# Transposing attention probabilities by DMA: the strided groups of three pairs of heads in mixer A

## The chip, the cores and the metric

The kernel runs on one core of one Trainium2 chip. The metric is the device time of one execution in microseconds (us), lower is better.

## The reference

A two-layer bidirectional encoder on x (1, 512, 1024) in float32. Layer 0 uses mixer A, layer 1 mixer B (latent attention); each mixer is followed by a squared-ReLU MLP of width 4096. The change is in mixer A, a mixture of dilated window attentions. One projection gives q, k and v for three groups (window, dilation) with eight heads of 128 each; the groups' outputs are merged by their softmax denominators:

```python
qkv = (h @ w_qkv).reshape(B, S, 3, N_GROUPS, A_HEADS, A_HEAD_DIM)
for g, (window, dil) in enumerate(((128, 1), (512, 4), (2048, 16))):
    q = rope(rms_norm(qkv[:, :, 0, g], q_gain[g]), S)
    k = rope(rms_norm(qkv[:, :, 1, g], k_gain[g]), S)
    o, lse = dilated_group(q, k, qkv[:, :, 2, g], window, dil)   # softmax(q k) v in the window
    ...
wts = jax.nn.softmax(jnp.stack(lses, 0), axis=0)
o = sum(wts[g][..., None] * outs[g] for g in range(3))
return o.reshape(B, S, A_WIDTH) @ w_o
```

## The kernel before, in words

Everything of one layer stays in the core's SBUF, with the 512 positions in four tiles of 128 partitions. The engines are TensorE (PE: matmuls and transposes into PSUM), VectorE (DVE), ScalarE (ACT), GpSimd (POOL) and SyncE (SP, which here issues DMA transfers). No order is written out by hand: a scheduler places each engine's instructions by a timeline of its own, and buffers come from pools, where a tile with a tag waits until one of the tag's buffers is free.

Projections are fp32 by parts. A weight tile is loaded raw (L146, L148), ScalarE takes the high part (whi, L158), VectorE the low part (wlo, L159), and TensorE adds three products (L186, the tiles called acc). These projections are the bulk of TensorE's work.

Mixer A handles its eight heads in four pairs b = 0 to 3. For a pair and a group, `project_in(b, g)` projects q and k of two heads. Each of its four tiles of 128 positions is squared (L138), rotated on VectorE (L278, L281), scaled (L130, POOL, L286, L287), and then transposed without TensorE: ScalarE splits its 32-bit words into low and high halves (L289), a DMA transpose issued by SP turns the 16-bit tile of 128 x 1024 (L292) into a tile xT (two buffers), and ScalarE puts the halves together again in qkT (L297). `scores(b, g)` then multiplies q and k (L578 and L582 for group 0, L589 for the strided groups 1 and 2), adds masks (L585, L594), takes maxima (L597, L598) and exponentials (L600), which leaves the probabilities P for each group and head.

When all three groups of a pair are there, `finish` runs `merge`, which works out the weights of the three groups with small matmuls (L644, L669) and multiplies the P tiles by them on VectorE (L675), and then `pv` for head h = 0 and 1. `pv` needs each P tile transposed, so that the key positions lie on the partitions. Before the change TensorE does that for all groups (L125, four 128x128 blocks into one PSUM tile tp). VectorE copies the tiles of groups 1 and 2 out (L685), ScalarE those of group 0 (L692), into tiles pT with four buffers:

```python
pT = aw.tile([P, 512], F32, tag="pT", name=nm("pT"), bufs=4)
V.tensor_copy(pT, tp)
```

Then TensorE multiplies them with the values: L699 for groups 1 and 2 (vt), L703 for group 0 (v0n and v0c), all into one PSUM tile sco, which VectorE copies to oT (L705). The values were written to DRAM earlier and are loaded pair by pair by `v_load` on SP: vt (L629), v0n (L605), and v0c in eight small transfers (L608).

So that TensorE has projections to do meanwhile, `finish(b)` is called after `project_in(b + 1, 0)`; the scheduler mixes the two, and the scores of the next pair's group 0, as its timeline has it. The last pair (b = 3) is finished apart, with the last head's value projection (`v_last`) and the start of the output projection as company; the tiles oA that the latter needs are split on ScalarE at L744.

Of the kernel before, what the change touches and what calls it, by code (L numbers as in the profile page):

```python
# [10 lines left out]
F32 = mybir.dt.float32  # L11
F32R = mybir.dt.float32r
U16 = mybir.dt.uint16
# [5 lines left out]
P = 128  # L19
S = 512  # L20
NT = S // P
# [3 lines left out]
HA = 8  # L25
# [63 lines left out]
def encoder_kernel(ctx: ExitStack, tc: tile.TileContext, x, norm_mix, norm_ffn, a_w_qkv, a_q_gain, a_k_gain,  # L89
                   a_w_o, b_w_in, b_q_a_gain, b_w_qb, b_kv_a_gain, b_w_kvb, b_q_gain, b_k_gain, b_w_o,  # L90
                   ffn_w1, ffn_w2, consts, out):
    nc = tc.nc
    V, A, G, PE = nc.vector, nc.scalar, nc.gpsimd, nc.tensor
# [3 lines left out]
    def nm(s):  # L97
        uid[0] += 1
        return f"{s}_{uid[0]}"
# [14 lines left out]
    tp_p = ctx.enter_context(tc.tile_pool(name="tp_p", bufs=2, space=PSUM))  # L114
# [9 lines left out]
    def transpose(o, i):  # L124
        PE.transpose(o, i, ident)  # L125
# [420 lines left out]
    with tc.tile_pool(name="apool", bufs=1, reuse_waits="tile") as ap_, \  # L546
# [19 lines left out]
        def scores(b, g, qkT, Pt, stats):  # L566

            m, den, nb = stats
            for h in range(2):
                qT, kT = qkT[:, h], qkT[:, 2 + h]  # L570
                for part in range(2 if g == 0 else 1):
                    sc = sc_p.tile([P, 512], F32, tag="sc", name=nm("sc"))
                    pt = Pt[g][h]
                    if g == 0:
                        for ii in range(2):
                            i = 2 * part + ii
                            q_i = qT[:, i * P:(i + 1) * P]
                            PE.matmul(sc[:, ii * 256:ii * 256 + 128], lhsT=q_i, rhs=kT[:, i * P:(i + 1) * P],  # L578
                                      start=True, stop=True)
                            segs = bass.AP(tensor=kT.tensor, offset=kT.offset + SEG_A[i],  # L580
                                           ap=[list(kT.ap[0]), [SEG_B[i] - SEG_A[i], 2], [1, 64]])
                            PE.matmul(sc[:, ii * 256 + 128:ii * 256 + 256], lhsT=q_i, rhs=segs, start=True, stop=True)  # L582
                        sv = sc.rearrange("p (i k) -> p i k", i=2)
                        pv = pt[:, 2 * part:2 * part + 2, :]
                        V.tensor_tensor(pv, sv, m0[:, 2 * part:2 * part + 2, :], op=ALU.add)  # L585
                        cols = range(2 * part, 2 * part + 2)
                    else:
                        for r in range(NT):
                            PE.matmul(sc[:, r * P:(r + 1) * P], lhsT=qT[:, r * P:(r + 1) * P],  # L589
                                      rhs=kT[:, r * P:(r + 1) * P], start=True, stop=True)  # L590
                        sv = sc.rearrange("p (i k) -> p i k", i=NT)
                        pv = pt
                        mk = (m1 if g == 1 else m2).unsqueeze(1).broadcast_to([P, NT, P])
                        V.tensor_tensor(pv, sv, mk, op=ALU.add)  # L594
                        cols = range(NT)
                    c0, c1 = cols[0], cols[-1] + 1
                    V.tensor_reduce(m[:, g, h, c0:c1], pv, axis=AX.X, op=ALU.max)  # L597
                    V.tensor_scalar(nb[:, g, h, c0:c1], m[:, g, h, c0:c1], -SCALE_A, None, op0=ALU.mult)  # L598
                    for c in cols:
# [77 lines left out]
        def pv(b, h, Pt, vt, v0n, v0c):  # L677
            pts = []
            hs = slice(DH * h, DH * h + DH)
            for g in (1, 2):  # L680
                tp = tp_p.tile([P, 512], F32, tag="tp", name=nm("tp"))
                for r in range(NT):
                    transpose(tp[:, r * P:(r + 1) * P], Pt[g][h][:, r])
                pT = aw.tile([P, 512], F32, tag="pT", name=nm("pT"), bufs=4)
                V.tensor_copy(pT, tp)  # L685
                pts.append(pT)
            for part in range(2):
                tp = tp_p.tile([P, 512], F32, tag="tp", name=nm("tp"))
                for i in range(NT):
                    transpose(tp[:, i * P:(i + 1) * P], Pt[0][h][:, i, part * P:(part + 1) * P])  # L690
                pT = aw.tile([P, 512], F32, tag="pT", name=nm("pT"), bufs=4)
                A.activation(pT.rearrange("p (i r j) -> p i r j", i=NT, r=NT),  # L692
                             tp.rearrange("p (i j r) -> p i r j", i=NT, r=NT), AF.Copy)
                pts.append(pT)
            o = sc_p.tile([P, 512], F32, tag="sc", name=nm("sco"))
            ov = o.rearrange("p (r m) -> p r m", r=NT)
            for r in range(NT):
                for g in (1, 2):
                    PE.matmul(o[:, r * P:(r + 1) * P], lhsT=vt[:, r, g - 1, hs], rhs=pts[g - 1][:, r * P:(r + 1) * P],  # L699
                              start=(r == 0 and g == 1), stop=False, skip_group_check=True)  # L700
            for i in range(NT):
                for part, vv in ((0, v0n), (1, v0c)):
                    PE.matmul(ov[:, :, 32 * i:32 * i + 32], lhsT=vv[:, i, hs], rhs=pts[2 + part][:, i * P:(i + 1) * P],  # L703
                              start=False, stop=(i == NT - 1 and part == 1), skip_group_check=True)
            V.tensor_copy(oT[:, 2 * b + h], o)  # L705
# [7 lines left out]
        def turned():  # L713
            return aw.tile([P, 8, P], U16, tag="xT", name=nm("xT"))
# [15 lines left out]
        for b in range(HA // 2):  # L730
            Pt = [[ap_.tile([P, NT, 256 if g == 0 else P], F32, tag=f"P{g}{h}", name=nm("P")) for h in range(2)]
                  for g in range(NG)]
# [223 lines left out]
    if True:  # L956
        with tc.tile_pool(name="bpool", bufs=1, reuse_waits="tile") as bp, \
# [205 lines left out]
            pend, tail, nxt, pT, pTs = [], [], None, None, None  # L1163
            plan = {2: [(kv_chunk, 0)], 3: [(kv_chunk, 1), (kv_chunk, 2)], 4: [(kv_chunk, 3), (q_chunk, 0)],
                    5: [(q_chunk, 1)], 6: [(q_chunk, 2)], 7: [(q_chunk, 3)]}
            for s_ in range(HB * NT + lag):
                p, c = divmod(s_, 8)
# [4 lines left out]
                if s_ >= lag:  # L1172
                    d, h2, r2, f = pend.pop(0)
                    if r2 == 0:
                        if pTs is None:
                            pTs = x16.tile([P, 2, NT, S], F32, tag="x16", name="pTs")
                        pT = pTs[:, h2]
# [54 lines left out]
```

## Time and profile before

| | us |
|---|---|
| median of 3 timed runs | 1414.49 (1411.01, 1414.49, 1415.36) |
| the profiled execution | 1413.8 |
| its span | 1412.0 |
| TensorE busy in the span | 1374.6 (97%) |
| VectorE busy | 940.3 (67%) |
| ScalarE busy | 801.3 (57%) |
| GpSimd busy | 225.9 (16%) |
| the four pairs of heads in mixer A | about 140 to 520 of the span |
| granted TensorE clock, mean | 0.999 |

An instruction is named by its line in the kernel. `out<-in` names the tiles, `xN` counts instructions or records, and an fp32 matmul leaves two records in the trace, a transpose one. In a table of groups the number after the bar is the busy time in us, then the mean in ns of one, then the idle time of the engine just ahead of them and what ended it (the releaser, after the arrow).

### The profile page before, as it was taken

To read this page: it belongs to the slowest core of one execution; us is meant where nothing else is said; L and a number is where in the kernel's file an instruction comes from. 1 tells how busy PE (TensorE), PEld (TensorE's weight loads), DVE (VectorE), ACT (ScalarE), POOL (GpSimd) and SP (SyncE) were. 2 spreads that over 40 slices of the span, in tenths; PEclk is the share of its full clock that TensorE was granted. 3 is DMA by queue.
4 is the path that set the end of the run, shared out by engine and by line. 5 is a ranking of instruction groups with operands and counts; after the bars stand their busy time and mean duration, and the time that the engine had idled before them with its cause. 6 is when DMAs were issued, how large, how long until landed. Compare 5 with 4: busy or idle time off the path is not lost.

```text
span 1412.0 us, 18967 instructions
## 1 busy us (share of the span) xinstructions
PE 1374.6 (97%) x6852; PEld 1166.0 (83%) x6852; DVE 940.3 (67%) x1497; ACT 801.3 (57%) x1642; POOL 225.9 (16%) x240
## 2 busy tenths in 40 slices
PE   7999999999999999999999999899999999999998
PEld 7999878888889889888888878776768888888886
DVE  6885778777788644564655768888644465574747
ACT  6544778687786625454536455777523553644543
POOL 1110212111122001020200204523101020020101
PEclk9999999999999999999999999999999999999999
DMA  9535554654555339486583934111116658393835
GB/s 320 166 136 165 125 132 103 163 135 115 147 131 129 110 120 261 139 185 175 122 236 90 236 88 94 60 30 31 45 45 192 167 125 232 96 234 118 201 83 120
DMA packets 171774, 197.83 MB, mean 140 GB/s; under 512 B 59104, under 2 KB 109024, under 8 KB 171680
## 3 DMA queue, kind: packets, MB, share of 16 engines
q1 hardware_dynamic: 152496, 157.55, 37.6%
q0 software_dynamic: 19184, 39.07, 15.4%
q8 instruction: 54, 0.88, 0.2%
q14 instruction: 40, 0.33, 0.1%
HBM read 176.13 MB, written 7.86 MB: 130 GB/s over the span
## 4 chain that ended last, share of the span: by engine, by line
PE 80%; DVE 7%; ACT 5%; DMA 4%; issue 2%; POOL 1%; SPq 0%; DVEq 0%; ACTq 0%; POOLq 0%
PE acc L186 46%; PE sc L857 11%; PE tp L857 7%; PE sc L423 3%; DMA xT<-t 3%; PE tp L125 3%; PE acc L1143 1%; PE sc L1037 1%; PE acc L1119 1%; PE tp L423 1%; DVE wlo L801 1%; PE acc L423 1%; DVE wlo L159 1%; PE sco L703 1%; PE sc L589 1%
## 5 line engine op out<-in xcount | busy, mean ns | idle before, releaser
L186 PE MATMUL acc<-whi,hT 128*128 128x512 f32 (+2 forms) x1216 | 378.7, 388 | 4.6 <-ACT hT L744 3.7
L186 PE MATMUL acc<-hT_f,whi 128*128 128x512 f32 (+1 forms) x1152 | 319.7, 367 | 1.7 <-DVE resid L920 1.2
L159 DVE TENSOR_TENSOR wlo<-raw,whi 128x1024 fp32r<-128x1024 f32 (+3 forms) x146 | 173.0, 1189 | 173.9 <-ACT whi L158 173.1
L186 PEld LDWEIGHTS acc<-whi,hT 128*128 128x128 f32 x1216 | 225.7, 188 | 45.6 <-ACT hT L744 4.2
L186 PEld LDWEIGHTS acc<-hT_f,whi 128*128 128x128 f32 x1152 | 209.0, 189 | 37.3 <-DVE resid L920 1.6
L158 ACT ACTIVATE whi<-raw 128x1024 fp32r<-128x1024 f32 (+3 forms) x146 | 149.3, 1028 | 154.0 <-PE acc L186 61.6
L186 PE MATMUL acc<-wlo,hT 128*128 128x512 f32 (+2 forms) x608 | 234.7, 387 | 0.2 <-DVE wlo L159 0.2
L801 DVE TENSOR_TENSOR wlo<-wqs,whi 128x1024 fp32r<-128x1024 f32 x112 | 137.9, 1232 | 110.3 <-ACT whi L800 110.3
L800 ACT ACTIVATE whi<-wqs 128x1024 fp32r<-128x1024 f32 x112 | 118.8, 1061 | 158.5 <-PE acc L186 66.2
L186 PE MATMUL acc<-hT_f,wlo 128*128 128x512 f32 (+1 forms) x576 | 205.4, 366 | 0.0
L857 PE MATMUL sc<-whi,asp 128*128 128x512 f32 x512 | 165.0, 390 | 0.8 <-DVE resid L831 0.7
L786 POOL DMA_DIRECT2D wqs<-in_ffn_w_dram x64 | 77.6, 1344 | 547.6 <-DVE wlo L801 366.3
L186 PEld LDWEIGHTS acc<-wlo,hT 128*128 128x128 f32 x608 | 114.4, 188 | 19.7 <-DVE wlo L159 0.3
L186 PEld LDWEIGHTS acc<-hT_f,wlo 128*128 128x128 f32 x576 | 108.9, 189 | 17.5
L857 PE MATMUL tp<-whi,asp 128*128 128x512 f32 x352 | 112.2, 390 | 1.8 <-DVE resid L831 1.8
L857 PEld LDWEIGHTS sc<-whi,asp 128*128 128x128 f32 x512 | 96.1, 188 | 21.5 <-issue 1.6
L133 POOL TENSOR_TENSOR qrs<-rs_v,nhalf 128x4 f32<-128x4 f32 x48 | 66.5, 1388 | 262.7 <-DVE rs_v L130 233.8
L857 PE MATMUL sc<-wlo,asp 128*128 128x512 f32 x256 | 99.7, 389 | 0.0
L297 ACT ACTIVATE qkT<-xT 128x1024 uint16<-128x1024 uint16 x48 | 56.5, 1182 | 42.5 <-DMA xT<-t 42.2
L857 PEld LDWEIGHTS tp<-whi,asp 128*128 128x128 f32 x352 | 66.1, 188 | 16.4 <-DVE resid L831 2.7
L857 PE MATMUL tp<-wlo,asp 128*128 128x512 f32 x176 | 68.2, 389 | 0.0
L831 DVE TENSOR_TENSOR resid<-resid,sc 128x512 f32<-128x512 f32 x64 | 43.1, 682 | 25.6 <-PE sc L857 25.6
(230 smaller groups left out, 2191.1 us busy)
## 6 DMA issues: line engine op xcount, KB each, us to landing
wqs<-in_ffn_w_dram SPq DMA_DIRECT2D x80, 512.0 KB, 5.2
raw<-in_ffn_w_dram SPq DMA_DIRECT2D x64, 512.0 KB, 4.4
wqs<-in_ffn_w_dram POOLq DMA_DIRECT2D x64, 512.0 KB, 7.3
raw<-in_a_w_qkv_dram SPq DMA_DIRECT2D x96, 256.0 KB, 3.3
b<-in_a_w_qkv_dram SPq DMA_DIRECT2D x24, 384.0 KB, 5.8
vall<-vo POOLq DMA_DIRECT2D x24, 192.0 KB, 2.3
raw<-in_a_w_o_dram SPq DMA_DIRECT2D x8, 512.0 KB, 3.7
raw<-in_b_w_o_dram SPq DMA_DIRECT2D x8, 512.0 KB, 3.8
```

Of the source, the lines that this page charges most:

```text
L125: PE.transpose(o, i, ident)
L133: G.tensor_tensor(out, v[:, :n], nhalf[:, :n], op=ALU.pow)
L158: A.activation(hi[:, :nk, :n], raw[:, :nk, :n], AF.Copy)
L159: V.tensor_tensor(lo[:, :nk, :n], raw[:, :nk, :n], hi[:, :nk, :n].bitcast(F32), op=ALU.subtract)
L186: PE.matmul(accs[o][:, oc], lhsT=lt, rhs=rt, start=(kt == 0 and p_i == 0 and hv == 0), stop=(kt == total - 1 and p_i == 2), skip_group_che ...
L297: A.activation(dst, xT.rearrange("p (h c) t -> p c t h", h=2), AF.Copy)
L423: PE.matmul(banks[t][:, :VH], lhsT=lt, rhs=rt[:, j], start=(first and k == 0 and i_ == 0), stop=(k == 3 and i_ == 2), skip_group_check=True)
L786: marks["sum"] = nc.gpsimd.dma_start(t, src, accum_op=ALU.add).ins
L800: A.activation(hi, x, AF.Copy)
L801: V.tensor_tensor(lo, x, hi.bitcast(F32), op=ALU.subtract)
L831: V.tensor_tensor(sl, sl, banks[t], op=op)
L857: PE.matmul(bk[t], lhsT=lt, rhs=rt[:, j], start=(first and k == 0 and i_ == 0), stop=(k == 3 and i_ == 2), skip_group_check=True)
```

## The change

For the first three pairs (b + 1 < 4) `pv` transposes the P tiles of groups 1 and 2 in the manner of the q/k path. VectorE copies the words' low halves and high halves into the two halves of a pT tile (128 x 1024 of 16 bits), SP issues a DMA transpose of it into an xT tile, and VectorE copies the halves from there into a second pT tile as whole words. The last pair keeps the old way, as does group 0 of every pair. The half-word tiles and the results share the tag pT with its four buffers, and xT is shared with the q/k path.

```diff
             for g in (1, 2):
-                tp = tp_p.tile([P, 512], F32, tag="tp", name=nm("tp"))
-                for r in range(NT):
-                    transpose(tp[:, r * P:(r + 1) * P], Pt[g][h][:, r])
                 pT = aw.tile([P, 512], F32, tag="pT", name=nm("pT"), bufs=4)
-                V.tensor_copy(pT, tp)
+                if b + 1 < HA // 2:
+                    words = Pt[g][h].rearrange("p r k -> p (r k)").bitcast(U16)
+                    halves = pT.bitcast(U16)
+                    V.tensor_copy(halves.rearrange("p (h n) -> p h n", h=2), words.rearrange("p (n h) -> p h n", h=2))
+                    xT = turned()
+                    nc.sync.dma_start_transpose(xT, halves)
+                    pT = aw.tile([P, 512], F32, tag="pT", name=nm("pT"), bufs=4)
+                    V.tensor_copy(pT.bitcast(U16).rearrange("p (c t h) -> p c t h", c=4, h=2),
+                                  xT.rearrange("p (h c) t -> p c t h", h=2))
+                else:
+                    tp = tp_p.tile([P, 512], F32, tag="tp", name=nm("tp"))
+                    for r in range(NT):
+                        transpose(tp[:, r * P:(r + 1) * P], Pt[g][h][:, r])
+                    V.tensor_copy(pT, tp)
                 pts.append(pT)
```

In the changed kernel the first copy is L685, the DMA transpose L687, the copy back L689; the old copy from PSUM is L695, ScalarE's copy L702, the matmuls with the values L709 (groups 1, 2) and L713 (group 0), and the copy to oT L715.

The scheduler places everything anew. On TensorE, at head 1 of the second pair, before (tp_3173 and tp_3180 are the transposed tiles of group 0, sco_3187 the output of head 1, acc_3509 a projection of the third pair; the eight transposes of groups 1 and 2 stand 20 rows further up):

```order
L186 MATMUL acc_3509<-whi_3520,hT_91 128x512
L186 MATMUL acc_3509<-wlo_3521,hT_91 128x512
L186 MATMUL acc_3509<-whi_3520,hT_91 128x512
L125 MATMUL tp_3173<-ck,P_2330 128x128 x4
L125 MATMUL tp_3180<-ck,P_2330 128x128 x4
L699 MATMUL sco_3187<-pT_3164,vt_2338 128x128
L699 MATMUL sco_3187<-pT_3171,vt_2338 128x128
```

And the same place after (tp_3165 and tp_3172 are the tiles of group 0, sco_3135 is head 0's output and sco_3179 head 1's, pT_3157 and pT_3163 are the two strided groups of head 1, sc_3220 and sc_3230 are scores of the third pair):

```order
L713 MATMUL sco_3135<-pT_3126,v0n_2335 128x4x32
L713 MATMUL sco_3135<-pT_3133,v0c_2336 128x4x32
L713 MATMUL sco_3135<-pT_3126,v0n_2335 128x4x32
L713 MATMUL sco_3135<-pT_3133,v0c_2336 128x4x32
L125 MATMUL tp_3165<-ck,P_2326 128x128 x3
L125 MATMUL tp_3172<-ck,P_2326 128x128 x4
L709 MATMUL sco_3179<-pT_3157,vt_2334 128x128
L578 MATMUL sc_3220<-qkT_2862 128x128
L582 MATMUL sc_3220<-qkT_2862 128x128
```

Head 1's first product with a strided group now follows head 0's last products and the transposes of group 0, with no projection between. After the rows shown come six more score matmuls, and then the first product with the second strided group. In the first pair ten passes of a projection stand ahead of that first product, in the third pair two.

On VectorE, at the same head of the same pair, before (pT_3164 and pT_3171 are the strided groups, oT the outputs of head 0 and head 1):

```order
L705 COPY oT<-sco_3141 128x512
L685 COPY pT_3164<-tp_3159 128x512
L685 COPY pT_3171<-tp_3166 128x512
L159 TENSOR_TENSOR wlo_3751<-raw_3747,whi_3750 128x1024
L585 TENSOR_TENSOR P_3205<-sc_3228,ca 128x512
L597 TENSOR_REDUCE stat_3211<-P_3205 128x2
L705 COPY oT<-sco_3187 128x512
```

And after (P_2328 and P_2330 are the strided groups, pT_3153 and pT_3159 their half words, pT_3157 and pT_3163 the results, P_3197 scores of the third pair):

```order
L685 COPY pT_3153<-P_2328 128x1024
L130 TENSOR_SCALAR rs_v_3601<-qss_3590 128x4
L130 TENSOR_SCALAR rs_v_3634<-qss_3623 128x4
L715 COPY oT<-sco_3135 128x512
L689 COPY pT_3157<-xT_3155 128x1024
L685 COPY pT_3159<-P_2330 128x1024
L585 TENSOR_TENSOR P_3197<-sc_3220,ca 128x512
L597 TENSOR_REDUCE stat_3203<-P_3197 128x2
L689 COPY pT_3163<-xT_3161 128x1024
```

The second group's copy to half words stands behind the first group's copy back. The first of these rows waits on TensorE: its buffer is one that head 0's last product but one with a strided group (L709) has read.

On the queue of SP, from the end of the second pair on, before (t_609, t_616 and t_623 are q/k tiles of the third pair's group 1, raw are weights, vt, v0n and v0c the values of the third pair):

```order
L292 DMA_TRANSPOSE xT_3412<-t_609_3401 128x8x128
L146 DMA raw_3809<-in_a_w_qkv_dram 128x2x256
L292 DMA_TRANSPOSE xT_3445<-t_616_3434 128x8x128
L292 DMA_TRANSPOSE xT_3478<-t_623_3467 128x8x128
L146 DMA raw_3816<-in_a_w_qkv_dram 128x2x256 x2
L629 DMA vt_3214<-vall_98 128x4x256
L629 DMA vt_3214<-vall_99 128x4x256
L605 DMA v0n_3215<-vall_97 128x4x256
L608 DMA v0c_3216<-vall_97 64x256 x8
L146 DMA raw_4149<-in_a_w_qkv_dram 128x2x256 x2
```

And after (t_610, t_617, t_624 and t_631 are the four q/k tiles of that group):

```order
L687 DMA_TRANSPOSE xT_3155<-pT_3153 128x8x128
L687 DMA_TRANSPOSE xT_3161<-pT_3159 128x8x128
L292 DMA_TRANSPOSE xT_3371<-t_610_3360 128x8x128
L292 DMA_TRANSPOSE xT_3404<-t_617_3393 128x8x128
L629 DMA vt_3206<-vall_98 128x4x256
L629 DMA vt_3206<-vall_99 128x4x256
L605 DMA v0n_3207<-vall_97 128x4x256
L608 DMA v0c_3208<-vall_97 64x256 x8
L292 DMA_TRANSPOSE xT_3437<-t_624_3426 128x8x128
L292 DMA_TRANSPOSE xT_3470<-t_631_3459 128x8x128
```

Head 1's two new transposes stand ahead of the q/k transposes of the next group, and two of those four now stand behind the eleven transfers of vt, v0n and v0c.

## The prediction

> **What bounds the kernel now.** I read the head of the profile page first, then the table by stretches for the part in which mixer A works on its pairs of heads, then the chain of work that ended last inside one of those stretches, and last the waits of TensorE there. The page:
>
> ```profile
> span 1412.0 us, 18967 instructions
> PE 1374.6 (97%) x6852; PEld 1166.0 (83%) x6852; DVE 940.3 (67%) x1497; ACT 801.3 (57%) x1642; POOL 225.9 (16%) x240
> PE 80%; DVE 7%; ACT 5%; DMA 4%; issue 2%; POOL 1%; SPq 0%; DVEq 0%; ACTq 0%; POOLq 0%
> ```
>
> The profiled execution took 1413.8 us, 1.8 around its span; the median of the three timed runs is 1414.49, 0.7 above it, so a sum made on the profiled execution carries over to the median within that. TensorE (PE) is busy for 97% of the span. Next the busy time by stretches: all of mixer A's pairs, then the ends of the first, second and third pair, where the changed function runs, and the end of the fourth. The columns are the stretch, its length, and the busy time of each engine.
>
> ```profile
> core 0: us, PE busy (x) PEld busy (x) DVE busy (x) ACT busy (x) POOL busy (x), PEclk, DMA share, GB/s
> 140.00:520.00 380.00, 372.84 (x2003) 321.44 (x2002) 282.68 (x560) 272.49 (x764) 66.53 (x48) 1.00 0.52 132
> 239.00:271.00 32.00, 30.22 (x183) 26.25 (x183) 24.08 (x42) 21.05 (x44) 4.84 (x4) 1.00 0.55 112
> 327.00:357.00 30.00, 30.00 (x187) 26.69 (x187) 21.61 (x35) 17.95 (x35) 5.57 (x3) 1.00 0.47 123
> 416.00:450.00 34.00, 34.00 (x205) 29.97 (x204) 28.66 (x54) 23.32 (x61) 11.96 (x7) 1.00 0.53 112
> 470.00:510.00 40.00, 36.29 (x218) 31.86 (x217) 21.65 (x41) 16.05 (x42) 0.00 (x0) 1.00 0.43 143
> ```
>
> Where the change works, TensorE stands still for 1.8 us in the first pair and not at all in the second and third, at a granted clock of 1.00. VectorE has 8.4 us of 30 free in the second pair and 5.3 of 34 in the third. So a matmul removed there is worth its full time, and a wait added there costs its full time. The chain through the end of the second pair (start, us, what) shows what stands one behind the other on TensorE; the number behind the x counts passes, two for an fp32 matmul and one for a transpose:
>
> ```profile
> 344.55 1.78 PE sco L703 x16
> 346.33 0.87 PE tp L125 x8
> 347.21 4.78 PE acc L186 x21
> 351.99 0.87 PE tp L125 x8
> 352.87 1.79 PE sco L699 x16
> 354.65 0.22 PE sc L578 x2
> ```
>
> Eight transposes of head 1's strided groups (346.33) are followed by 21 passes of the projection, 4.78 us, in which VectorE takes the transposed tiles out of PSUM. That is the cover that the old way has. The waits that TensorE does have in these pairs and their tail:
>
> ```profile
> PE acc L186 <- ACT hT L744: 3.7, 2, 2.3
> PE sco L703 <- ACT pT L692: 1.6, 1, 1.6
> PE sc L589 <- ACT qkT L297: 1.6, 1, 1.6
> PE acc L186 <- DVE wlo L159: 0.2, 1, 0.2
> ```
>
> **The change part by part.** *Removed from TensorE:* 48 transposes, in 12 groups of four (two strided groups, two heads, three pairs). Eight took 0.87 us above, so a group is 0.435 and the sum is 12 x 0.435 = **-5.2 us**, all of it on a busy TensorE.
>
> *Added: a chain through the SP queue.* Each group now needs a copy on VectorE into half words (L685), a DMA transpose (L687), and a copy back (L689). What the nearest rows say of the price of a copy:
>
> ```profile
> L685 DVE COPY pT<-tp 128x512 f32<-128x512 f32 x16 | 10.5, 682 | 0.6 <-PE tp L125 0.6
> L1122 DVE TENSOR_SCALAR bmx<-bmx,rqs 128x1 f32<-128x1 f32 x32 | 6.5, 206 | 0.3
> L159 DVE TENSOR_TENSOR wlo<-raw,whi 128x1024 fp32r<-128x1024 f32 x51 | 62.1, 1220 | 34.6 <-ACT whi L158 34.4
> ...
> L1126 DVE TENSOR_SCALAR pe<-pe,bmx x32: 469/486/1041, 913.2 to 1039.1; 128x512 f32<-128x512 f32 x32
> ```
>
> No row has a copy of 1024 half words on VectorE. L1126 reads one SBUF tensor of 512 elements in 486 ns (median) and the one-element L1122 takes 206, so an element costs (486-206)/511 = 0.55 ns, and 1024 of them 206 + 1023 x 0.55 = 0.77. I take 0.75 us. The lower end is 0.49 (as long as 512 words, if half the bytes count), the upper 1.22 (L159, 1024 elements with two sources). And the price of a DMA transpose of the same size, from the one that the q/k path has (first and second row: issue on the SP queue, ns, and issue to landing), with one of them in the chain of the first pair:
>
> ```profile
> L292 SPq DMA_TRANSPOSE xT<-t x48: 1232/1238/1897, 147.0 to 460.3; - x48
> ...
> DMA to landing us min/median/max: 3.0/3.2/5.7
> ```
>
> ```profile
> 262.48 0.02 issue
> 262.50 3.22 DMA xT<-t
> 265.72 0.02 issue
> ```
>
> So one group takes 0.75 + 3.2 + 0.75 and some 0.1 of hand-overs: 4.8 us. [...]
>
> In head 0 the two chains run behind the projection: between the first group's and the second group's first use 22 to 26 passes of L186 and eight transposes stand (5.9 us or more), and over 30 passes ahead of the first. I cost it at nothing; without that cover it would be 4.8 a group. In head 1 it is different, because of three things in the new order. The half words and the results share the four pT buffers, so head 1's first L685 waits until head 0's L709 has read one. On VectorE the second group's L685 stands behind the first group's L689, so the two DMA transposes go one after the other. And the new order puts little projection behind it. The chain from head 0's last L709 but one to head 1's last copy is 2 x 4.8 = 9.6 us. TensorE's cover, by the rows above (0.22 an fp32 matmul, 0.109 a transpose, 4.78/21 = 0.228 a projection pass):
> - pair 0: L709 0.22, eight L713 1.78, eight transposes 0.87, ten projection passes 2.28, L709 0.22, eight score matmuls 1.78: 7.15, short by 2.45 (the first half, 5.15, covers its 4.8);
> - pair 1: 0.22 + 1.78 + 0.87 + 0.22 + 1.78 = 4.87, short by 4.73;
> - pair 2: 0.22 + 1.78 + 0.33 + 0.46 + 0.22 + 1.78 = 4.79, short by 4.81.
>
> Together 12.0 us of new standstill. The old wait at the same place goes; it is the 1.62 us ahead of this row of the first pair (start, duration, then the idle time before it):
>
> ```profile
> 268.39 0.49 PE L703 MATMUL sco<-pT,v0n 128*128 128x128 f32 x2 [1.62 <-ACT pT L692]
> ```
>
> What is late next there is the copy on ScalarE (now L702), which the longer wait for L689 hides. So the chain costs **+10.4 us**. With copies at 0.49 it would be 3 x 4 x 0.26 = 3.1 less, with copies at 1.22 it would be 5.6 more.
>
> *VectorE's work:* 24 x 0.75 - 12 x 0.68 = 9.8 us more, 3.3 a pair. The first pair's 7.9 idle us of 32 hold it in sum, but the low parts of the weights (L159) stand behind it, and TensorE already waited once for one (0.2). I take **+0.7**, between 0 and 3.
>
> *The queue of SP and VectorE's own:* L687 waits on SP for L685, and L292 of the next group's q/k, the loads of the next pair's values and the weights stand behind it; on VectorE each L689 waits some 3 us for its transpose with the next pair's L585, L281 and L287 behind it. The loads that the q/k transposes now partly follow:
>
> ```profile
> 270.62 2.11 SPq L629 DMA_DIRECT2D vt<-vall  x2
> 272.82 0.57 SPq L605 DMA_DIRECT2D v0n<-vall  x1
> 273.49 6.85 SPq L608 DMA_DIRECT2D v0c<-vall  x8
> ```
>
> In the second pair two of the four q/k transposes are now behind these 9.5 us. Two waits of 3 us and 3.3 of extra work are 9.3 a pair, against the 8.4 and 5.3 that VectorE had idle plus the 4.7 by which the stretch grows: it just fits. TensorE has at its side 61 projection passes, 13.9 us, before it needs that group. I take **+1**, between 0 and 3 a pair.
>
> *The tail* is written as before, but the scheduler now puts 70 instead of 26 of the last value projection's matmuls ahead of the last merge's second product (L669), and two instead of 26 projection passes between head 0's transposes and their use. There two copies of 0.68 lie bare, 1.4 less what the two leave, and the wait of 3.7 for L744 may shrink. I take **+1**, between -2 and +3.
>
> The sum is -5.2 + 10.4 + 0.7 + 1 + 1 = +7.9, and 1413.8 + 7.9 = **1421.7 us**. With the bounds of the cheap copies and of the tail it reaches down to about 1417, and up to 1425 with ordinary copies.
>
> **The rivals.** *R1, faster: there is no standstill.* The chain fits under the 4.8 us of cover if 4 x 0.75 + 2d + 0.2 is no more, d being a landing, so from d = 0.8 down. Then the transposes go, the old wait of 1.6 with them, and only the weights and the tail remain: -5.2 - 1.6 + 0.7 + 1 = -5.1, 1408.7 us. Against it stands the least landing of 48, 3.0; for it only that those landings may hold a queue's waiting. [...]
>
> *R2, slower copies.* VectorE moves half words with a step of two at the price of L159, 1.22. The chain costs 5.6 more and late weights 2: 1429.3 us. For it: ScalarE's and VectorE's rows of 1024 elements are all over 1 us; against it: the single-source row L1126.
>
> *R3, the queue decides.* The next group's scores wait for late q/k transposes, 3 us a pair instead of 1 for all three: 1429.7. It decides once the 9.5 us of loads and the two chained transposes together outlast the 13.9 us of projection; 9.5 + 4.8 is 14.3, so it is close where ScalarE adds its own copy.
>
> *R4, about no change: the wait is given back.* While TensorE stands, ScalarE and VectorE get ahead, and the waits on L744 (3.7) and for q/k (1.6) vanish: 1421.7 - 5.3 = 1416.4. For it: these engines are idle a quarter of the time and more; against it: the wait on L744 is in the tail, 20 us and more behind the last changed pair, with a chain of its own.
>
> That the change would not do what it says is excluded by the new order, which has the 12 DMA transposes and 24 copies.
>
> **How the numbers follow.** About 0.3%, 4.2 us, is what a measurement of this kernel can tell from no change; same is 1409.6 to 1418.0. My forecast has 0.39, of which 0.04 falls below 1418; R1 0.15 (faster), R2 0.14 and R3 0.12 (slower), R4 0.20 (same). That makes slower 0.35 + 0.14 + 0.12 = 0.61, same 0.24, faster 0.15. The range runs from 1413, below R4, to 1430, just above R2 and R3, and leaves out R1. The forecast's own range is 1417 to 1425.
>
> **What would show it right or wrong.** In the changed profile: TensorE waiting for L689 at L709 in head 1, twice in pairs 1 and 2 (about 1.9 and 2.8 us) and once in pair 0 (2.4), 12 us together; L689 and L685 at about 0.75; landings of L687 at 3.2; no wait of TensorE for L689 in head 0; 0 to 3 us of new waits for L297 or L159. It is wrong if the standstill at L709 is under 8 us or over 16, if copies take over 1 us, if head 0 waits too, or if new waits stand in the tail beyond 3 us.

## The result, and the profile after

The changed kernel takes 1421.83 us (median of six runs, 1421.22 to 1426.37) against 1413.76 of the kernel before (six runs beside it). The ratio is 1.0064, with a 95% interval of 1.0051 to 1.0077: the change makes the kernel slower by 0.6%. The profiled execution after took 1421.8 us, 8.0 more than the one before. Its head:

```profile
span 1420.0 us, 18902 instructions
...
PE 1375.6 (97%) x6804; PEld 1162.3 (82%) x6804; DVE 948.2 (67%) x1509; ACT 802.2 (56%) x1642; POOL 230.6 (16%) x240
```

The 48 transposes are gone (6852 to 6804 records), and yet TensorE is busy for 1.0 us more than before. It stands idle for 1420.0 - 1375.6 = 44.4 us instead of 37.4. Its waits in mixer A after the change, in the form in which those of before were shown (us in total, times, longest):

```profile
PE sco L709 <- DVE pT L689: 6.4, 4, 2.3
PE sc L578 <- DVE P L585: 2.3, 3, 0.8
PE acc L186 <- ACT hT L754: 1.0, 1, 1.0
PE acc L186 <- ACT whi L158: 0.9, 1, 0.9
PE scm L644 <- DVE P L594: 0.6, 1, 0.6
PE acc L186 <- DVE wlo L159: 0.5, 1, 0.5
PE sc L589 <- ACT qkT L297: 0.5, 2, 0.3
```

The largest is the one that was forecast, L709 behind the copy back L689, and all four of its cases lie in head 1. The old wait of L703 has gone, those on L744 (now L754) and for q/k have shrunk. The second row is new and was not foreseen: of the eight score matmuls put between the two strided groups, the last four wait for VectorE to empty a score tile (L585), 0.78 us in each pair. The timeline of TensorE at head 1 of the second pair (start, duration, instruction, then the idle time before it and what ended it):

```profile
345.96 0.93 PE L125 MATMUL tp<-ck,P 128*128 128x128 f32 x7
349.21 0.49 PE L709 MATMUL sco<-pT,vt 128*128 128x128 f32 x2 [2.33 <-DVE pT L689]
349.54 0.39 PE L578 MATMUL sc<-qkT 128*128 128x128 f32 x2
...
351.82 0.80 PE L578 MATMUL sc<-qkT 128*128 128x128 f32 x2 [0.78 <-DVE P L585]
...
353.77 3.27 PE L709 MATMUL sco<-pT,vt 128*128 128x128 f32 x14
```

and of the third pair:

```profile
438.62 0.49 PE L709 MATMUL sco<-pT,vt 128*128 128x128 f32 x2 [1.77 <-DVE pT L689]
...
440.79 0.49 PE L578 MATMUL sc<-qkT 128*128 128x128 f32 x2 [0.78 <-DVE P L585]
...
443.16 1.83 PE L709 MATMUL sco<-pT,vt 128*128 128x128 f32 x14 [1.22 <-DVE pT L689]
```

and of the first pair, where there is one wait for L689:

```profile
265.15 1.83 PE L709 MATMUL sco<-pT,vt 128*128 128x128 f32 x14 [1.04 <-DVE pT L689]
```

The same 14 passes take 1.83 us in the first and third pair and 3.27 in the second. The table by stretches shows why; the column before the last two is the granted clock:

```profile
344.00:348.00 4.00, 2.88 (x27) 2.64 (x25) 1.63 (x4) 1.31 (x8) 1.98 (x2) 1.00 0.60 72
348.00:352.00 4.00, 2.00 (x11) 1.71 (x12) 2.18 (x4) 0.60 (x1) 0.00 (x0) 0.75 0.28 53
352.00:356.00 4.00, 4.00 (x18) 3.84 (x19) 3.33 (x8) 2.75 (x6) 0.00 (x0) 0.50 0.70 132
356.00:360.00 4.00, 4.00 (x32) 3.93 (x31) 3.63 (x8) 3.10 (x6) 0.00 (x0) 0.90 0.42 118
```

After the standstill of 2.33 us the clock was halved: 4 x (0.25 + 0.50 + 0.10) = 3.4 us of full clock are missing, which is 6.8 us at half. Not all of it is added to the time, because a part of it stands where TensorE would have waited. VectorE's second copy back in this pair ends at 353.02 + 0.69 = 353.71, and the second strided group starts on TensorE at 353.77, right behind it:

```profile
353.02 0.69 DVE L689 COPY pT<-xT 128x1024 uint16<-128x1024 uint16 x1 [0.53 <-DMA xT<-pT]
```

Between 349.21 and 353.77 stand nine fp32 matmuls, 9 x 0.22 = 2.0 us at full clock. The chain would therefore have held TensorE for 4.56 - 2.0 = 2.6 us there at full clock too (an estimate), of which only the 0.78 for L585 is recorded as a wait. The 3.0 us at half clock behind 353.77, 1.5 us lost, come on top.

Added up over the whole trace in stretches of 4 us, the changed kernel lost 5.1 us to half clock, all of it in mixer A: 3.4 here and 1.7 between 480 and 488, in the tail. (The clock of 0.79 in its last stretch, from 1416 on, cost nothing, as TensorE has no matmul behind 1416.3.) The kernel before lost none in mixer A and 1.7 between 1072 and 1080, in layer 1, where the changed one lost none. The difference is 3.4 us. (The mean clocks of the two spans, 0.996 and 0.999, would give 1420 x 0.004 - 1412 x 0.001 = 4.3, but they are rounded to 0.001, which is 1.4 us.) The half clock in layer 1 does not hang on the change: the profiled executions of result_in_P and copies_only below show it there too (granted clock 0.74 from 1095 to 1100, and 0.74 from 1080 to 1085), those of the change and of own_xT do not, and in 66 other executions of the kernel before the mean clock lies between 0.995 and 1.000. The rows behind mixer A show the same: up to 1073 they come 9.4 to 9.6 us later than before (the last row of L920, now L930, starts at 1083.1 instead of 1073.5), and near the end 8.3.

The chain itself, from the chain of work that ended last in the third pair (start, us, what):

```profile
434.08 0.70 DVE pT L685
...
434.80 3.05 DMA xT<-pT
...
437.87 0.69 DVE pT L689
438.57 0.60 DVE pT L685
...
439.20 3.19 DMA xT<-pT
...
442.41 0.70 DVE pT L689
```

Copy, transpose, copy back, and then the second group the same way, one after the other, 9.0 us from 434.08 to 443.1. And the new lines by themselves (ns, least, median and most; then issue to landing in us):

```profile
L685 DVE COPY pT<-P x12: 679/685/695, 239.1 to 438.5; 128x1024 uint16<-128x1024 uint16 x12
...
L689 DVE COPY pT<-xT x12: 679/690/696, 244.3 to 442.4; 128x1024 uint16<-128x1024 uint16 x12
...
L687 SPq DMA_TRANSPOSE xT<-pT x12: 1231/1237/1241, 239.8 to 439.2; - x12
...
DMA to landing us min/median/max: 3.0/3.2/3.9
```

### The profile page after: what moved, and what is told of

Read it like the earlier page. It is cut to its first block, busy times and chain, and to the rows that moved or that the text cites. A ratio compares the mean times of both kernels' runs of the same rounds, so it can differ in the third digit from the quotient of the medians.

```text
span 1420.0 us, 18902 instructions
## 1 busy us (share of the span) xinstructions
PE 1375.6 (97%) x6804; PEld 1162.3 (82%) x6804; DVE 948.2 (67%) x1509; ACT 802.2 (56%) x1642; POOL 230.6 (16%) x240
## 4 chain that ended last, share of the span: by engine, by line
PE 75%; DVE 10%; ACT 6%; DMA 4%; issue 3%; POOL 1%; SPq 0%; DVEq 0%; ACTq 0%; POOLq 0%
PE acc L186 41%; PE sc L867 11%; PE tp L867 7%; PE sc L423 3%; DMA xT<-t 2%; PE tp L125 2%; PE acc L1153 1%; PE sc L1047 1%; PE acc L1129 1%; DVE wlo L159 1%; PE tp L423 1%; ACT P L600 1%; DVE wlo L811 1%; PE sco L709 1%; DMA xT<-pT 1%
## 5 line engine op out<-in xcount | busy, mean ns | idle before, releaser
L159 DVE TENSOR_TENSOR wlo<-raw,whi 128x1024 fp32r<-128x1024 f32 (+3 forms) x146 | 172.7, 1188 | 153.2 <-ACT whi L158 152.8
L186 PEld LDWEIGHTS acc<-hT_f,whi 128*128 128x128 f32 x1152 | 208.2, 189 | 37.4 <-DVE resid L930 1.6
L158 ACT ACTIVATE whi<-raw 128x1024 fp32r<-128x1024 f32 (+3 forms) x146 | 149.5, 1029 | 153.2 <-PE acc L186 60.8
L133 POOL TENSOR_TENSOR qrs<-rs_v,nhalf 128x4 f32<-128x4 f32 x48 | 72.2, 1519 | 269.4 <-DVE rs_v L130 246.7
L297 ACT ACTIVATE qkT<-xT 128x1024 uint16<-128x1024 uint16 x48 | 56.3, 1181 | 34.7 <-DMA xT<-t 34.4
L138 ACT ACTIVATE junk<-acc 128x128 f32<-128x128 f32 x192 | 52.3, 272 | 15.1 <-PE acc L186 11.4
```

What stands on the lines that cost most here:

```text
L133: G.tensor_tensor(out, v[:, :n], nhalf[:, :n], op=ALU.pow)
L138: A.activation(junk, x, AF.Square, scale=1.0 / math.sqrt(dim), accum_out=out)
L158: A.activation(hi[:, :nk, :n], raw[:, :nk, :n], AF.Copy)
L159: V.tensor_tensor(lo[:, :nk, :n], raw[:, :nk, :n], hi[:, :nk, :n].bitcast(F32), op=ALU.subtract)
L186: PE.matmul(accs[o][:, oc], lhsT=lt, rhs=rt, start=(kt == 0 and p_i == 0 and hv == 0), stop=(kt == total - 1 and p_i == 2), skip_group_che ...
L297: A.activation(dst, xT.rearrange("p (h c) t -> p c t h", h=2), AF.Copy)
```

## The experiments

After the result the theory was **A**: the loss is head 1's chain, which starts late because half words and results share the pT buffers, runs its two transposes one after the other and has little projection to hide behind. The rivals: **B**, VectorE's 24 copies make weights and q/k tiles late; **C**, the SP queue does, with the value loads and the q/k transposes behind the new transposes; **D**, the new order of the tail. The fall of A brought two more: **E**, the new transposes share the two xT buffers with the q/k path; **F**, VectorE stands at L689 until a transpose has landed, with the next group's q/k work placed behind it.

All ratios are to the kernel before, run beside each kernel (its medians there were 1413.3 to 1414.9). "Idle" is the span less TensorE's busy time, "clock" the span times what the mean granted clock falls short of 1, both in the profiled execution; as the mean is rounded to 0.001, "clock" can be off by 0.7 us.

| kernel | us | ratio (95% interval) | idle | clock |
|---|---|---|---|---|
| before | 1413.8 | 1 | 37.4 | 1.4 |
| the change | 1421.8 | 1.0064 (1.0051 to 1.0077) | 44.4 | 5.7 |
| result_in_P | 1434.0 | 1.0143 (1.0128 to 1.0159) | 51.9 | 10.0 |
| own_half_word_tile | 1424.0 | 1.0068 (1.0053 to 1.0083) | 45.1 | 5.7 |
| shadow_chain | 1439.0 | 1.0180 (1.0164 to 1.0196) | 54.2 | 7.2 |
| head_0_only | 1415.9 | 1.0009 (0.9999 to 1.0018) | 39.5 | 1.4 |
| copies_only | 1417.8 | 1.0030 (1.0017 to 1.0042) | 37.5 | 2.8 |
| transposes_only | 1415.7 | 1.0016 (1.0005 to 1.0027) | 37.8 | 4.2 |
| result_in_P_values_on_pool | 1443.6 | 1.0209 (1.0190 to 1.0228) | 59.0 | 15.9 |
| before_values_on_pool | 1413.1 | 0.9992 (0.9981 to 1.0002) | 36.9 | 0.0 |
| own_xT | 1417.1 | 1.0030 (1.0019 to 1.0041) | 40.8 | 4.2 |
| copy_back_on_pool | 1427.9 | 1.0102 (1.0088 to 1.0116) | 50.7 | 7.1 |
| own_xT_copy_back_on_pool | 1420.6 | 1.0050 (1.0038 to 1.0062) | 44.1 | 7.1 |
| change_with_own_xT | 1426.2 | 1.0079 (1.0066 to 1.0093) | 47.3 | 7.1 |

### Taking the standstill away

`result_in_P` needs no second pT tile:

```diff
-                    pT = aw.tile([P, 512], F32, tag="pT", name=nm("pT"), bufs=4)
+                    pT = Pt[g][h].rearrange("p r k -> p (r k)")
                     V.tensor_copy(pT.bitcast(U16).rearrange("p (c t h) -> p c t h", c=4, h=2),
```

> The change as it is, but VectorE copies the turned words back into the P tile that they came from, not into a new pT tile. Nothing is left out. So head 1's half words need no buffer that head 0's products have to read first, and in the new order 21 passes of the projection (two to eight of them in the first pair, with eight transposes and 17 products) stand ahead of head 1's first product. If the chain behind the shared buffers is the cause (theory A), the 8.7 us of standstill at L709 and beside it go and so does the half clock behind it: 5.2 us of transposes are saved, the tail stays as it is in the changed kernel, and the time is 1407 to 1411 us, 3 to 7 under the kernel before. If VectorE's 24 copies are the cause (B) or the SP queue with the loads behind the new transposes (C), nothing of these is changed and it stays at 1419 to 1423. If the new order of the tail is the cause (D), it also stays above 1417.

Measured 1434.0. TensorE's waits in mixer A in this kernel:

```profile
PE sc L589 <- ACT qkT L297: 8.0, 5, 3.1
PE acc L186 <- ACT hT L754: 3.5, 2, 2.6
PE tp L125 <- DVE P L675: 2.1, 2, 1.9
```

The wait of L709 for L689 is gone, as A wanted, but the time did not fall, it rose by 12 us over the change. In its place stands the wait of rival R3 of the prediction, for q/k tiles. Its chain at the second pair's end:

```profile
353.84 1.23 SPq L292
...
355.18 0.58 SPq L629
355.80 0.62 SPq L629
...
356.47 6.71 DMA v0n<-vall
...
363.74 3.12 DMA xT<-t
...
366.89 1.18 ACT qkT L297
...
368.12 0.49 PE sc L589 x2
```

The last of the four q/k transposes (landing from 363.74 on) stood on SP behind the value loads issued from 355.18, and TensorE waited 3.1 us for it. A as the only cause has fallen.

`own_half_word_tile` takes the same wait away in another manner:

```diff
-                pT = aw.tile([P, 512], F32, tag="pT", name=nm("pT"), bufs=4)
...
-                    halves = pT.bitcast(U16)
+                    halves = aw.tile([P, 512], F32, tag="pH", name=nm("pH"), bufs=1).bitcast(U16)
```

> The change as it is, but the half words have a tag of their own with one buffer, and the four pT tiles hold results only. Head 1's first chain can then start as soon as the single half-word tile is read by the transpose before; the two chains still go one after the other. Theory A: the start no longer waits for head 0's products, nine to 20 passes of projection stand in the chain's shadow, and most of the standstill goes: 1408 to 1413. B, C and D: 1419 to 1423, as the copies, the queue and the tail are what they were.

Measured 1424.0: A's forecast missed by 11 us and more. Idle time is as in the change, 45.1, with the wait for q/k at 4.6 us and 3.4 for L130 in place of the 6.4 for L689.

### The parts alone

`head_0_only` has the change for h == 0:

```diff
-                if b + 1 < HA // 2:
+                if b + 1 < HA // 2 and h == 0:
```

> The change for head 0 alone: six of the 12 groups are transposed by DMA, head 1's by TensorE as before. Theory A: head 0's chain lies behind the projection, so half of the transposes are saved, 2.6 us, without a standstill: 1409 to 1413, the tail's order apart. B or C: half of the loss, 1416 to 1419.

Measured 1415.9, which cannot be told from no change. The 2.6 us of transposes were saved and given back: idle rose by 2.1 us, and the wait for ScalarE's copies of group 0 (L713, before the change L703) doubled from 1.6 to 3.2 us, in five cases. Neither forecast met it; A's was missed by 3 us, that of B and C nearly held.

`shadow_chain` adds the whole chain to the kernel before, and nobody reads its result:

```diff
                 V.tensor_copy(pT, tp)
                 pts.append(pT)
+                if b + 1 < HA // 2:
+                    pH = aw.tile([P, 512], F32, tag="pH", name=nm("pH"), bufs=1)
+                    words = Pt[g][h].rearrange("p r k -> p (r k)").bitcast(U16)
+                    halves = pH.bitcast(U16)
+                    V.tensor_copy(halves.rearrange("p (h n) -> p h n", h=2), words.rearrange("p (n h) -> p h n", h=2))
+                    xT = turned()
+                    nc.sync.dma_start_transpose(xT, halves)
+                    V.tensor_copy(pH.bitcast(U16).rearrange("p (c t h) -> p c t h", c=4, h=2),
+                                  xT.rearrange("p (h c) t -> p c t h", h=2))
```

> The kernel before, with TensorE's transposes and VectorE's copies out of PSUM kept, and the whole new chain added beside them for the same 12 groups: 24 copies of half words on VectorE and 12 DMA transposes on SP, into a tile that nobody reads. Extra work only, the output is made the old way. Theory A: nobody waits for the chain, so it costs what VectorE and the queue cost when hidden, 0 to 3 us over the kernel before, 1414 to 1417. Theory B or C: VectorE has even 8 us more to do than in the changed kernel and SP the same transposes, so the loss of 8 us shows here as well or more, 1421 and up.

Measured 1439.0, 24 us more, where A allowed 3. In this kernel the copy back is L694; its row, and the row that says what ended VectorE's idle time ahead of it (us, times):

```profile
L694 DVE COPY pH<-xT x12: 686/695/695, 245.8 to 450.3; 128x1024 uint16<-128x1024 uint16 x12
...
  DMA xT<-pH: 17.9, 9
```

VectorE stood for 17.9 us at landings, and TensorE waits for what VectorE and ScalarE do next:

```profile
PE acc L186 <- DVE t L281: 5.8, 3, 3.1
PE acc L186 <- ACT hT L753: 5.8, 2, 4.8
PE sc L589 <- ACT qkT L297: 3.4, 5, 1.2
```

No product of TensorE depends on the chain here, so the chain costs through what it shares with the q/k path: VectorE's order, the SP queue and the landing buffers. The 24 us are more than the change itself loses (8.1) and saves on transposes (5.2) together, so this run shows that the chain is dear beside the q/k path, and not how much of it the changed kernel pays. The next two take it apart. `copies_only` has only the copies, `transposes_only` only the transposes, both added behind the same old copies:

```diff
+                    for _ in range(2):
+                        pH = aw.tile([P, 512], F32, tag="pH", name=nm("pH"), bufs=1)
...
+                        V.tensor_copy(halves.rearrange("p (h n) -> p h n", h=2), words.rearrange("p (n h) -> p h n", h=2))
```

> The kernel before with 24 more copies of 1024 half words on VectorE (two behind each of the 12 old copies out of PSUM), into a tile that nobody reads; no DMA transpose. Extra work only. The chain alone (A) has fallen: with head 1's standstill gone the time rose to 1434, and the whole chain as a shadow cost 24 us. Left are VectorE's time (B), the SP queue with what stands behind the new transposes (C), and the two xT buffers that both kinds of transposes share (E). B: 24 x 0.69 = 16.6 us of VectorE come out late as weights and q/k tiles: 1424 to 1436. C or E: VectorE hides it, 1413 to 1419.

```diff
+                if b + 1 < HA // 2:
+                    nc.sync.dma_start_transpose(turned(), Pt[g][h].rearrange("p r k -> p (r k)").bitcast(U16))
```

> The kernel before with 12 more DMA transposes on SP, of the P tiles as they are, into xT tiles that nobody reads; no copy on VectorE. Extra work only. C or E: the q/k transposes wait behind the new ones, for the queue or for a free xT buffer, 1422 to 1436. B: 1413 to 1418.

Measured 1417.8 and 1415.7: the copies cost 3.8 us, the transposes 1.7 over the kernel before beside them (1413.98). Neither explains 24, nor do both together. So B and C as plain loads on an engine or a queue are small; what is left is that one waits for the other, in a new order.

### The queue, the landing buffers and VectorE's wait

`result_in_P_values_on_pool` moves the value loads to GpSimd's queue, and `before_values_on_pool` does so without the change:

```diff
-                nc.sync.dma_start(vt[:, :, g - 1, :n], vall[g].rearrange("(m r) d -> m r d", r=NT)
+                nc.gpsimd.dma_start(vt[:, :, g - 1, :n], vall[g].rearrange("(m r) d -> m r d", r=NT)
```

> result_in_P with one more edit: the loads of the values for groups 1 and 2 and for group 0 (three lines, 11 transfers a pair) are issued by GpSimd's queue and no longer stand in SP's. Nothing is left out. In result_in_P a q/k transpose stood behind 8.5 us of them, and TensorE waited 3.1 us for it at 368. C: the waits for L297 go, 8 us and the half clock behind them: 1416 to 1424. If only the loads were in the way and neither VectorE nor xT is short: under 1413. B or E: 1430 to 1436.

> The control for the run beside it: the kernel before with the same loads on GpSimd's queue. No theory gives it more than the 1.6 us of the one wait for L297, which stands ahead of the first pair's end: 1411 to 1416.

Measured 1443.6 and 1413.1. The control does nothing, and the edit makes result_in_P 10 us slower. The wait for L297 fell to 0.9 us there, but TensorE waited 13.1 us for L585 (longest 9.4), and the slowest q/k transpose landed after 14.4 us where it was 5.2. The long wait hangs on that landing: VectorE's rotation (L281) waited 10.6 us for a landing at the longest, VectorE did nothing from 366 to 374 and TensorE nothing from 370 to 378. C's forecast failed: taking the loads off SP's queue did not help. But GpSimd, whose queue now issues the 11 transfers of the values, was busy all the time from 360 to 364, and the DMA engines moved 129 to 282 GB/s from 360 to 374, so that these transfers slowed the transpose itself is not excluded.

`own_xT` is result_in_P with a landing tile of its own:

```diff
-                    xT = turned()
+                    xT = aw.tile([P, 8, P], U16, tag="xP", name=nm("xP"), bufs=1)
```

> result_in_P with one more edit: the new transposes land in a tile of their own (one buffer) and no longer in the two xT buffers of the q/k path. Nothing is left out. Copies alone cost 3.8 us and transposes alone 1.7, together as a chain 24, so it is the coupling: either by the shared xT buffers (E), or because VectorE, which takes its instructions in order, stands at L689 until a transpose has landed, with the q/k work of the next group behind it, and SP at L687 until VectorE has copied (F). E: the q/k transposes no longer wait for L689 to empty a buffer, and the time falls from 1434 to 1410 to 1418. F: L689 stands on VectorE as before, 1426 to 1436.

Measured 1417.1, 17 us less than result_in_P and inside the forecast of E. TensorE's largest waits are now

```profile
PE sc L589 <- ACT qkT L297: 3.5, 4, 1.2
PE acc L186 <- DVE wlo L159: 2.9, 2, 1.9
PE acc L186 <- DVE rs_v L130: 1.4, 1, 1.4
```

and L709 waits 0.2 us for L689. VectorE itself stood idle for 6.0 us at landings ahead of L689 here, against 3.4 in result_in_P, and the kernel is faster all the same; that speaks against F. It is the fastest of the kernels that have all 12 groups by DMA, and still 0.3% slower than before.

`copy_back_on_pool` is the change with L689 on GpSimd, `own_xT_copy_back_on_pool` the same on own_xT:

```diff
-                    V.tensor_copy(pT.bitcast(U16).rearrange("p (c t h) -> p c t h", c=4, h=2),
+                    G.tensor_copy(pT.bitcast(U16).rearrange("p (c t h) -> p c t h", c=4, h=2),
```

> The change as it is, with the copy back (L689) on GpSimd in place of VectorE; all else, shared pT and shared xT too, as in the changed kernel. Nothing is left out. F: VectorE stands at no landing any more and has 8 us less to do; GpSimd's copy is slower (an estimate of 1.5 to 3 us from its rows of over 1 us for four elements), which the 20 passes of projection that the new order puts there hide: 1410 to 1418. E or the serial chain (A): no better than the change, 1420 to 1432.

> Both edits together on result_in_P: a landing tile of their own, and the copy back on GpSimd. Nothing is left out. E or F, whichever is the cause, gives its gain here: 1408 to 1414. If this stays above 1420, neither is the cause, and the loss lies with SP's order or the new order as a whole.

Measured 1427.9 and 1420.6, both slower than with VectorE (1421.8 and 1417.1), though a copy took GpSimd only 1.16 us in the median and no product waited for it. F's forecast was missed by 10 us: moving the copy back off VectorE does not help the change. The run does not part F cleanly, though, because GpSimd now stood for 42.1 us at landings, and it too has a part of the q/k path (L133) in its order. The second missed its 1408 to 1414 as well and lies above the 1420 from which on its expectation held neither E nor F for the cause, although own_xT, with the same landing tile, had met E's forecast. So E's gain is not had in every order.

`change_with_own_xT` makes the same edit as own_xT on the change itself, which keeps the shared pT tiles.

> The change as it is, pT tiles shared by half words and results too, with one edit: the new transposes land in a tile of their own (one buffer), not in the two xT buffers of the q/k path. Nothing is left out. Head 1's first copy still waits for head 0's product and the two chains still go one after the other, but the new order puts 27, 33 and 34 passes of projection ahead of head 1's first product. E: the shared landing buffers are what the change loses by, and this gives the time that own_xT had, 1413 to 1419, 3 to 9 under the change. If the pT tiles (A) matter beside it, it stays at 1420 or above.

Measured 1426.2, no faster than the change. L709 waits 1.2 us for L689 here instead of 6.4, and again others take the place:

```profile
PE sc L589 <- ACT qkT L297: 5.9, 5, 3.0
PE acc L186 <- DVE wlo L159: 3.3, 3, 1.7
PE sc L589 <- DVE P L585: 3.0, 1, 3.0
```

So the two shared tiles make a square: both shared 1421.8, only the result in P 1434.0, only the landing tile apart 1426.2, both apart 1417.1. Each edit alone makes it worse, the two together make it better. E alone has fallen for the change as well. Every edit also makes the scheduler order all engines anew, and the runs do not part an edit's own worth from that of the order that came with it. What stays open is how much each single coupling carries; what is shown is that parting one of the two tiles alone gains nothing. D, the order of the tail, had no run of its own; the waits there are given below.

## Why the prediction was right, point by point

The forecast was 1421.7 us, slower, and 1421.8 was measured. The direction came from the mechanism that was forecast; that the number agrees to 0.1 us is luck. By its steps:

- **Transposes.** 48 records are gone, and a pass of those that are left still takes 0.11 us (five in 0.55); -5.2 stands.
- **Price of a copy.** 0.69 us measured, 0.75 taken. R2 (1.22 us) is out. VectorE's busy time rose by 7.9 us, 9.8 were reckoned.
- **Price of a transpose.** 3.2 us in the median, as the q/k path has it, and never under 3.0. R1, which needed landings of 0.8 us or less, is out.
- **The chain.** Its place, its serial form and its length (9.0 measured, 9.6 reckoned) were right, and head 0 does not wait, as costed at nothing. Its size was not what was said: the prediction called itself wrong if the standstill at L709 was under 8 us, and 6.4 are recorded there, in one, one and two waits for the three pairs where one, two and two were forecast. With the 2.3 us for L585 at the score matmuls between the groups it is 8.7 of the 12.0. With the 1.8 us that half clock hides in the second pair (2.6 less the recorded 0.78) it is an estimated 10.5: 1.8, 4.9 and 3.8 us for the three pairs where 2.45, 4.73 and 4.81 were reckoned. A good part of what is left over is the shorter chain, 0.6 us a pair.
- **What was missing** is the clock. The prediction had no term for it. It lost 5.1 us in mixer A, of which the 1.8 just named would have been standstill at full clock.
- **Weights** (+0.7): the waits for L158 and L159 went from 0.2 to 1.4 us. **Queue** (+1): the wait for L297 fell from 1.6 to 0.5, so in the change itself R3 cost nothing. **Tail** (+1): the waits in the tail are L754 1.0, L644 0.6, 0.5 and 0.3 for L695 and 0.3 for L702, 2.7 together where L744 had 3.7, but half clock came there too (1.7 us lost between 480 and 488).
- **R4**, the wait given back: it happened in part. The waits for L744 and L297 shrank by 2.7 and 1.1 us, 3.8 of the 5.3 forecast, against which stand the 5.1 us of half clock.

The sum came out right because errors cancel. As recorded, the prediction's own terms give -5.2 + (8.7 - 1.6) + 1.2 - 1.1 - 1.0 = +1.0 where +7.9 was forecast, or an estimated +2.8 with the standstill that half clock hides. The rest of the 8.0 is none of its terms. All in all the profiles give -5.2 for transposes, +7.0 of idle time and +3.4 of clock, +5.2 of the 8.0. Part of the other 2.8 is that the first matmul behind a wait took longer: from its start to that of the next 0.33 us (349.21 to 349.54 above), and 0.33, 0.33 and 0.32 behind the waits at 262.95, 438.62 and 440.79, where 0.22 is usual. Mixer A has 17 waits of TensorE after the change and had five before, which makes an estimated 12 x 0.11 = 1.3 us. The last 1.5 were not traced to rows. Chance has a share too: of the two profiled executions only the one before had the 1.7 us of half clock in layer 1.

One thing the prediction implied and the runs contradict: it treated the terms as a sum, by which the change without its standstill would have been a gain (R1 at 1408.7). Where the standstill was taken away, in result_in_P, own_half_word_tile, copy_back_on_pool and (but for 1.2 us) change_with_own_xT, the time was 1424 to 1434; in own_xT it was 1417.1 and in own_xT_copy_back_on_pool 1420.6, still slower than before. A reading that fits is that SP, ScalarE and VectorE catch up with the next group's q/k while TensorE stands at L709, and that without the standstill TensorE meets them later: the waits that took its place are those for L297, L130, L159 and L585. This is argued from these waits; no run parts it from the new order that came with each edit. The standstill is where the loss shows in the change, and was rightly found there, but its size is not what its removal gains.

## What to carry to other kernels

A transfer that replaces a few matmuls is priced by its whole chain: the copies on both ends, the landing, and who stands in order behind each wait; here 0.435 us of TensorE a group was traded for 4.5 us of chain. Cover is counted in the new order, from the instruction that frees the buffer to the first use, and it was the count that told the sign. Taking away the wait that the profile shows is no proof of what it is worth: let the added work run beside the old kernel with nobody reading it (24 us here), and then its parts alone (3.8 and 1.7), before blaming one of them. Half clock behind a wait can hide another wait (an estimated 1.8 us in the second pair here), so the two are not simply added.

## What the runs showed of the hardware that had not been expected

Half clock came behind short standstills. After the change it came behind one of 2.33 us (granted clock 0.50 in every us from 350 to 356), in own_xT behind one of 1.91 (0.59 from 336 to 340). In the tail of the changed kernel it came behind waits of 0.35 and 0.56 us within 2 us (0.89 and 0.69 in the two stretches from 480 on); eight passes of the short matmuls L644, 1.06 us, stand right behind those waits, so the waits alone are not shown to be enough. It did not come at 436 to 443 in the changed kernel, with 3.8 us of standstill in three parts (1.00 from 436 to 444). At 476 the kernel before stood for 2.27 us, waiting for L744, and kept the full clock (1.00 from 472 to 484), while transposes_only stood for 2.1 at the same place and lost it (0.62 from 476 to 480). So length alone does not decide; what does was not shown.
